# A hybrid gMLP and dilated-attention block on eight cores: reloading V in 5 transfers instead of 32 per head pair, with early weight loads gated by x and a reordered gating stage

## The chip, the cores and the metric

The kernel runs on all 8 cores of one Trainium2 chip. Each core does one of the 8 sequences of the batch with the same program; the cores exchange nothing. The metric is the device time of the slowest core in microseconds (us).

In these runs the program had a fast state and a slow one. In the slow state the cores of one die, or of both, showed a lower granted TensorE clock and the run took longer.

## The reference, cut to what matters

```python
# one block: x (8, 2048, 1024); 16 heads of 64; 8 gating groups of 128 channels; FF width 4096
h   = rms_norm(x, g1)
[u | v | q | k | v_attn | gate_a | gate_b] = h @ w_in
ya  = gelu(u) * (tril(W_s) @ layer_norm(v) + b_s)         # by chunks of 128 tokens
yb  = mixture of 3 dilated causal windows (128,1) (512,4) (2048,16) with ALiBi,
      weighted by their softmax denominators
m   = sigmoid(gate_a) * (ya @ w_a) + sigmoid(gate_b) * (yb @ w_b)
x1  = x + rms_norm(m @ w_o, g2);  out = x1 + rms_norm(relu(rms_norm(x1, g3) @ w1)**2 @ w2, g4)
```

(The activation and gate forms are abridged.) The three windows need V with the keys on the partitions in three different orders. The kernel projects V once per two head pairs, stores it in DRAM, and reads it back in two more orders: V0 for dilation 1, V1 for dilation 4. Dilation 16 uses the order in which it was projected.

## The kernel before

A helper records all operations; a scheduler orders them for each engine by priorities and by a cost given to each operation. That is why nearly all TensorE work has one line in the profile, and why new cost numbers move instructions.

The store of V and the reload for a head pair, 16 + 16 transfers of 48 KB:

```python
vscr_d = nc.dram_tensor("v_scr", [4, 128, 16, 384], BF16).ap()
...
P.dma("sp", lambda e, q=q: e.dma_start(out=vscr_d[pr][:, 4 * q:4 * q + 4, :], in_=stg[d][...]), ...)
...
def load_v(hp, prio):
    d, pr, hh = hp % 2, hp // 2, hp % 2
    src = vscr_d[pr]
    for a in range(4):
        s = src.rearrange("(n m) (c a) x -> a m c n x", n=4, a=4)[a]
        for c in range(4):       # V1: 16 transfers
            fns.append(... out=V1[d][32 * a:32 * a + 32, 4 * c:4 * c + 4, :], in_=s[:, c, :, 192 * hh:192 * hh + 192] ...)
    P.dma("sp", fns, 786e3, f"v1_{d}", rd, [V1[d].key()], prio=prio)
    s0 = src.rearrange("(b m) t x -> b t m x", m=8)
    for b in range(16):          # V0: 16 transfers
        fns.append(... out=V0[d][:, b, :], in_=s0[b][:, :, 192 * hh:192 * hh + 192] ...)
    P.dma("sp", fns, 786e3, f"v0_{d}", rd, [V0[d].key()], prio=prio)
```

The weights of the last MLP are turned into bf16 while attention runs: 24 transfers from DRAM to DRAM, 8 of w1 (2 MB in, 1 MB out) and 16 of w2 (half of that each). They are dealt evenly by number over the 32 slots of attention (8 head pairs times 4):

```python
for f in range(8):
    its.append(... P.dma("pool", ... dma_start(out=w1s_d[f], in_=w1_d[f]) ..., after=P.ops[-1]))
for f in range(16):
    its.append(... P.dma("pool", ... dma_start(out=w2s_d[f], in_=w2_d[f]) ..., after=P.ops[-1]))
...
for _ in range((nconv * (4 * hp + c + 1)) // 32 - (nconv - len(conv))):
    conv.pop(0)()
```

The softmax here doesn't subtract the row's maximum and nothing guards it: scores larger than these inputs give would overflow.

## Time and profile before

Before the change the median of three runs was 1358.19 us (1352.44 to 1365.54). The profiled run took 1348.16 us. It was one of the quicker ones. Its slowest core is core 5 with a span of 1346.6 us; the cores span 1323.8 to 1346.6 us.

| what (before, slowest core) | us |
|---|---|
| TensorE busy | 1191.2 of 1346.6 |
| TensorE waits for V from DRAM | 43.1 |
| start, until the QK projection of the last tiles begins (mean of cores) | 72.9 |
| one wait for the gating's reload | 15.9 |
| output projection stage (mean of cores) | 149.4 |

The page of the kernel before, first the TensorE line of the busy times (busy us, share, instructions; PEld is the weight load), then the chain of work that ended last, by engine:

```profile
PE 1191.2 (88%) x7560; PEld 601.9 (45%) x7560; DVE 563.9 (42%) x1007; ACT 483.9 (36%) x857; POOL 59.2 (4%) x122
PE 67%; DMA 13%; SPq 6%; DVE 5%; issue 5%; ACT 3%; DVEq 0%; ACTq 0%; POOL 0%; POOLq 0%
```

TensorE bounds the kernel, but a fifth of the chain is transfers and the queue that issues them (SPq). The waits of TensorE, kernel before (what it did next, what it waited for: total us, times, longest):

```profile
PE pst L195 <- DMA sb_V_0_50<-v_scr: 36.4, 3, 20.0
PE pst L199 <- DVE sb_xn_92 L486: 16.4, 4, 7.9
PE pst L195 <- DMA sb_gc<-gc_scr: 15.9, 1, 15.9
PE pst L195 <- DVE sb_xo_148 L926: 8.4, 2, 6.6
PE pst L195 <- DMA sb_V_1_51<-v_scr: 6.7, 1, 6.7
PE pst L195 <- DMA sb_w_6_144<-w_bf: 4.8, 1, 4.8
```

Two lines are waits for V (43.1 us). They ended at 122, 168, 228 (the one of 20.0 us) and 378 us. The issuing queue of the kernel before, from its timeline (start us, us from first to last issue, engine, line, operation, count). Line 577 is V1, line 583 is V0; the first two rows belong to head pair 0, the last two to head pair 2:

```profile
101.44 8.29 SPq L577 DMA_DIRECT2D sb_V_0_52<-v_scr  x16
109.78 10.43 SPq L583 DMA_DIRECT2D sb_V_0_50<-v_scr  x16
181.58 34.72 SPq L577 DMA_DIRECT2D sb_V_0_52<-v_scr  x16
216.35 9.91 SPq L583 DMA_DIRECT2D sb_V_0_50<-v_scr  x16
```

For head pair 0 the 32 issues take 19 us and V0 was usable at 122. For head pair 2 sixteen issues took 35 us: something else held the queue up. The reload also waits for the stores of V that it reads. The last of them before head pair 2 was issued at 154.6 us and landed only 26.8 us later (KB, us from issue to landing):

```profile
v_scr<-sb_stgV_49 SPq DMA_DIRECT2D x1, 384.0 KB, 26.8
```

### The profile page before, as it was taken

Reading aid. Unit: us, or ns where it says so; the run is one execution under the profiler, and the core shown is the slowest. Engines: PE = TensorE matmul, PEld = TensorE weight load, DVE = VectorE, ACT = ScalarE, POOL = GpSimd, SP = SyncE. Lnnn points to the kernel's source line nnn. Section 1 sums busy time; section 2 is a strip of 40 time slices with the busy share of each in tenths; the row PEclk is TensorE's granted clock in tenths of the full one; section 3 lists DMA queues with packets and bytes.
Section 4 is the critical chain, followed back from the end, with each engine's and each line's share of the span. In section 5 each row is a group of like instructions: output and inputs, shape, how many; then the busy total and the mean of one; then the engine's idle time right before and its main releaser. Section 6 shows DMA issues by size and latency. Waiting matters only on the chain.

```text
span 1346.6 us, 20587 instructions; the slowest of 8 cores (1323.8 to 1346.6 us)
## 1 busy us (share of the span) xinstructions
PE 1191.2 (88%) x7560; PEld 601.9 (45%) x7560; DVE 563.9 (42%) x1007; ACT 483.9 (36%) x857; POOL 59.2 (4%) x122
## 2 busy tenths in 40 slices
PE   2587794999967997799999996998999999999997
PEld 1264462666534433444444442443444444444443
DVE  3545662777745651643223235683122122212212
ACT  3524562666756523121222224574113213212311
POOL 0000000000000221000000011000000000000000
PEclk9798996999978999899999997998999999999999
DMA  9334986866774468221311129455010021011001
GB/s 226 108 88 86 120 137 117 165 138 125 141 147 72 102 169 168 64 64 32 63 32 32 32 78 349 167 182 193 32 64 32 0 79 47 1 63 63 1 32 63
DMA packets 67109, 130.44 MB, mean 97 GB/s; under 512 B 40641, under 2 KB 40769, under 8 KB 64450
## 3 DMA queue, kind: packets, MB, share of 16 engines
q0 software_dynamic: 9536, 54.53, 20.8%
q1 hardware_dynamic: 57474, 74.59, 18.9%
q8 instruction: 62, 1.02, 0.3%
q14 instruction: 37, 0.30, 0.1%
HBM read 139.58 MB, written 44.04 MB: 136 GB/s over the span
## 4 chain that ended last, share of the span: by engine, by line
PE 67%; DMA 13%; SPq 6%; DVE 5%; issue 5%; ACT 3%; DVEq 0%; ACTq 0%; POOL 0%; POOLq 0%
PE pst L195 66%; SPq L577 4%; DMA v_scr<-sb_stgV_49 3%; DMA gc_scr<-sb_gct_123 2%; SPq L583 2%; DMA gc_scr<-sb_gct_125 2%; DMA sb_xt_89<-x 2%; DMA sb_xo_148<-x 1%; DVE sb_ybT L705 1%; DMA sb_V_0_50<-v_scr 1%; PE pst L199 1%; DMA sb_gc<-gc_scr 1%; DMA x_scr<-sb_xo_148 1%; DMA v_scr<-sb_stgV_48 1%; DMA sb_w_6_144<-w_bf 1%
## 5 line engine op out<-in xcount | busy, mean ns | idle before, releaser
L195 PE MATMUL pst<-sb_w_146,sb_hid 128*128 128x512 bf16 x1024 | 221.7, 379 | 2.7 <-issue 1.4
L195 PEld LDWEIGHTS pst<-sb_w_146,sb_hid 128*128 128x128 bf16 x1024 | 100.0, 98 | 124.0 <-issue 3.7
L968 ACT ACTIVATE sb_hid<-pst 128x512 bf16<-128x512 f32 x128 | 76.4, 597 | 136.5 <-PE pst L195 135.9
L969 DVE TENSOR_TENSOR sb_hid<-sb_hid 128x512 bf16<-128x512 bf16 x128 | 54.2, 424 | 144.8 <-ACT sb_hid L968 142.1
L982 ACT ACTIVATE sb_junk_162<-pst 128x512 bf16<-128x512 f32 x32 | 19.1, 597 | 197.6 <-PE pst L195 197.6
L629 ACT ACTIVATE sb_Et_82<-pst 128x1024 bf16<-128x1024 f32 (+1 forms) x54 | 52.0, 962 | 65.7 <-PE pst L195 59.0
L195 PE MATMUL pst<-sb_hT,sb_wqk_62 128*128 128x512 bf16 x256 | 67.0, 412 | 4.9 <-ACT sb_hT L496 2.7
L195 PE MATMUL pst<-sb_wout,sb_merged 128*128 128x512 bf16 x256 | 60.4, 391 | 8.4 <-DVE sb_xo_148 L926 8.4
L629 ACT ACTIVATE sb_Et_84<-pst 128x1024 bf16<-128x1024 f32 (+1 forms) x53 | 51.2, 965 | 39.4 <-PE pst L195 33.6
L195 PE MATMUL pst<-sb_wva,sb_hT 128*128 128x512 bf16 x256 | 59.8, 393 | 5.5 <-ACT sb_gv_121 L782 4.7
L195 PE MATMUL pst<-sb_hT,sb_wqk_63 128*128 128x512 bf16 x256 | 62.9, 391 | 0.4 <-DVE sb_stgV_49 L561 0.2
L629 ACT ACTIVATE sb_Et_83<-pst 128x1024 bf16<-128x1024 f32 (+1 forms) x53 | 51.8, 977 | 24.9 <-PE pst L195 18.9
L195 PE MATMUL pst<-sb_hT,sb_wg_129 128*128 128x512 bf16 x256 | 57.9, 379 | 0.0
L195 PE MATMUL pst<-sb_hT,sb_wg_130 128*128 128x512 bf16 x256 | 57.9, 379 | 0.0
L195 PEld LDWEIGHTS pst<-sb_wout,sb_merged 128*128 128x128 bf16 x256 | 25.1, 100 | 39.9 <-issue 13.9
L195 PEld LDWEIGHTS pst<-sb_wva,sb_hT 128*128 128x128 bf16 x256 | 25.3, 101 | 38.1 <-issue 11.7
L195 PEld LDWEIGHTS pst<-sb_hT,sb_wqk_62 128*128 128x128 bf16 x256 | 24.6, 104 | 38.9 <-issue 18.8
L826 ACT ACTIVATE sb_yaT<-pst 128x512 bf16<-128x512 f32 x32 | 18.9, 599 | 56.6 <-PE pst L195 56.6
L195 PEld LDWEIGHTS pst<-sb_hT,sb_wg_130 128*128 128x128 bf16 x256 | 25.0, 98 | 30.2
L195 PEld LDWEIGHTS pst<-sb_hT,sb_wg_129 128*128 128x128 bf16 x256 | 25.0, 98 | 30.0
L195 PEld LDWEIGHTS pst<-sb_hT,sb_wqk_63 128*128 128x128 bf16 x256 | 23.6, 100 | 29.9 <-issue 7.1
L878 ACT ACTIVATE sb_sg_0_134<-pst,sb_small 128x512 f32<-128x512 f32 x16 | 11.0, 687 | 71.9 <-PE pst L195 71.9
(389 smaller groups left out, 1910.4 us busy)
## 6 DMA issues: line engine op xcount, KB each, us to landing
w_bf<-w POOLq DMA_DIRECT2D x8, 1024.0 KB, 17.7
w_bf<-w POOLq DMA_DIRECT2D x16, 512.0 KB, 9.0
sb_w_146<-w_bf POOLq DMA_DIRECT2D x16, 512.0 KB, 21.3
sb_xo_148<-x SPq DMA_DIRECT2D x8, 512.0 KB, 4.7
sb_gc<-gc_scr SPq DMA_DIRECT2D x16, 256.0 KB
sb_xo_149<-x SPq DMA_DIRECT2D x8, 512.0 KB, 4.8
sb_wg_129<-w_g POOLq DMA_DIRECT2D x4, 1024.0 KB, 8.5
sb_wg_130<-w_g POOLq DMA_DIRECT2D x4, 1024.0 KB, 8.2
```

The source lines that it names most:

```text
L195: e.matmul(out, lhsT=l, rhs=r, start=st, stop=sp, skip_group_check=True))
L199: fns = [lambda e, a=a, b=b: e.transpose(out=a, in_=b, identity=ident) for a, b in outs_ins]
L577: fns.append(lambda e, a=a, c=c, s=s: e.dma_start(out=V1[d][32 * a:32 * a + 32, 4 * c:4 * c + 4, :], in_=s[:, c, :, 192 * hh:192 * hh + 192]))
L583: fns.append(lambda e, b=b: e.dma_start(out=V0[d][:, b, :], in_=s0[b][:, :, 192 * hh:192 * hh + 192]))
L629: P.act(lambda e: e.activation(out=et[:, :, 0:W], in_=psall[:, sb:sb + 2, 0:W], func=AF.Exp, scale=0.125), 2 * W, [], [et.key()], [sb, sb ...
L705: P.dve(lambda e, hh=hh, lo=lo: e.tensor_tensor(out=ybT[lo:lo + 64, hp, 512 * c:512 * c + 512], in0=psr(bks[hh], lo, lo + 64), in1=lr[lo:l ...
L826: P.act(lambda e, bk=bk, g=g, w=w: e.activation(out=yaT[:, g, 512 * w:512 * w + 512], in_=ps(bk), func=AF.Gelu_apprx_tanh), 512, [], [yaT. ...
L878: P.act(lambda e, j=j, cb=cb, po=po, s_=s_: e.activation(out=s_[j][:], in_=ps(po + j), func=AF.Tanh, scale=0.5, bias=small[:, bg_c + 8 * j ...
L968: P.act(lambda e, fb=fb, bk=bk: e.activation(out=hid[:, fb, :], in_=ps(bk), func=AF.Relu), 512, [], [hid.key(fb)], [bk])
L969: P.dve(lambda e, fb=fb: e.tensor_tensor(out=hid[:, fb, :], in0=hid[:, fb, :], in1=hid[:, fb, :], op=ALU.mult), 512, [hid.key(fb)], [hid.k ...
L982: P.act(lambda e, hf=hf, bb=bb, s_=s_: e.activation(out=junk4[:, 0:512], in_=ps(bb[hf]), func=AF.Square, accum_out=s_[:, 8 + hf:9 + hf]), ...
```

## The change

It has four parts. The intent of each:

1. **V.** The scratch layout in DRAM changes so that V0 is read in 4 transfers and V1 in 1. The key orders inside a block change with it (`kk0`, `k1`), so the reordering copies of K and the bias tables do too; the copies into KT1 (K in the order for dilation 4) move from VectorE to ScalarE. V0 is loaded first.
2. **Start.** Eight x buffers instead of five; two of the early weight loads and the first bias table wait for x tiles; all copies of the transposed x (hT) go to VectorE.
3. **Output projection.** Each w2 load waits for a tile of the output projection; w1 slice 6 gets a place that frees earlier.
4. **Order.** New cost numbers; conversions and bias loads tied to a slot's last product (`anchor`); the first gating products one group later; the reload of V gets another priority.

The diff, cut to its core:

```diff
-            cost += max(n / 2400.0 + 0.0025, 0.1 if slow else 0.03)
+            cost += max(n / 2400.0 + 0.0025, 0.055) * (0.55 if slow else 1.0)
   ... (other cost numbers of ScalarE, VectorE and the queues likewise)
-    vscr_d = nc.dram_tensor("v_scr", [4, 128, 16, 384], BF16).ap()
+    vscr_d = nc.dram_tensor("v_scr", [4, 4, 128, 4, 384], BF16).ap()
   ...
+    NX, NXN = 8, 4            # x and normalised-x buffers, were 5 and 3
   ...
-    load_wv(0, -1970.0)
-    load_wqk(1, -1900.0)
+    load_wv(0, -1970.0, gate[5])
+    load_wqk(1, -1900.0, gate[13])
   ...
-            its.append(lambda f=f: P.dma("pool", ... w1s_d[f] ..., after=P.ops[-1]))
+            its.append(lambda f=f: P.dma("pool", ... w1s_d[f] ..., after=anchor[0]))
   ...
-                    P.dve(lambda e, o1=o1, s=s: e.tensor_copy(out=o1, in_=s.rearrange("p (a n m) -> p a n m", a=4, n=4)), ...
+                    P.act(lambda e, o1=o1, s=s: e.activation(out=o1, in_=s, func=AF.Copy), 512, [kk],
+                          [KT1[d].key((512 * w, 512 * w + 512))])
   ...
-        (load_v: 16 + 16 transfers, shown above)
+        src = vscr_d[pr].rearrange("c m a x -> (c m a) x")[:, 192 * hh:192 * hh + 192]
+        s0 = src.rearrange("(c b q) x -> c q b x", c=4, q=32)
+        P.dma("sp", [lambda e, c=c: e.dma_start(out=V0[d][32 * c:32 * c + 32, :, :], in_=s0[c]) for c in range(4)], 786e3, f"v0_{d}", rd,
+              [V0[d].key()], prio=prio)
+        P.dma("sp", lambda e: e.dma_start(out=V1[d][:], in_=src.rearrange("(b p) x -> p b x", p=128)), 786e3, f"v1_{d}", rd, [V1[d].key()],
+              prio=prio + 1)
   ...
-            P.prio = U0 + 10 * g + 5 + n4
+            P.prio = U0 + 10 * g + (5 if g else 21) + n4
   ...
-    W1OFF = [160, 168, 192, 144, 152, 128, 176, 184]
+    W1OFF = [160, 168, 192, 144, 152, 128, 136, 184]
   ...
-              [P.nkey(("w2s", q))], [w2.key((2 * q, 2 * q + 2))], prio=F0 + 20 + q)
+              [P.nkey(("w2s", q))], [w2.key((2 * q, 2 * q + 2))], prio=F0 + 20 + q, after=fgate[q])
```

More of the change, by code (lines that the diff above doesn't have):

```diff
@@ L200, in tr, with act @@
         return self._add("pe", fns, 0.06 * len(fns), reads, [self.bank(b) for b in banks], prio, lat=0.17, name=name)
-    def act(self, fn, n, reads, writes, banks=(), prio=None, name=""):
-        return self._add("act", [fn], 0.2 + n / 1200.0, reads, list(writes) + [self.bank(b) for b in banks], prio, lat=0.04, name=name)
+    def act(self, fn, n, reads, writes, banks=(), prio=None, name="", acc=False):
+        return self._add("act", [fn], (0.4 if acc else 0.11) + n / 1200.0, reads, list(writes) + [self.bank(b) for b in banks], prio, lat=0.04, name=name)
     def dve(self, fn, n, reads, writes, banks=(), prio=None, name="", rate=1):
-        return self._add("dve", [fn], 0.065 + n / (960.0 * rate), reads, list(writes) + [self.bank(b) for b in banks], prio,
+        return self._add("dve", [fn], 0.09 + n / (960.0 * rate), reads, list(writes) + [self.bank(b) for b in banks], prio,
                          lat=0.04, name=name)
@@ L214, in dma @@
             fns = [fns]
-        cost = (0.06 if q != "pool" else 1.0) * len(fns)
+        cost = (0.45 if q != "pool" else 0.7) * len(fns)
         o = self._add(q, list(fns), cost, reads, writes, prio, nb=nbytes, chan=chan, lat=2.0, name=name)
@@ L433, in build_nc @@
     Lr = [buf(f"Lr{i}", (199 + 2 * i) * K, [512], F32) for i in range(2)]
-    xt = [buf(f"xt{i}", (165 + 4 * i) * K, [1024], F32) for i in range(5)]
-    xn = [buf(f"xn{i}", (185 + 2 * i) * K, [1024]) for i in range(3)]
-    junk = buf("junk", 193 * K, [1024])
-    gbc = buf("gbc", 199 * K, [1024], F32)
-    grow = buf("grow", 195 * K, [1024], F32)
-    ones1 = buf("ones1", 203 * K, [128], F32)
+    NX, NXN = 8, 4
+    xt = [buf(f"xt{i}", (165 + 4 * i) * K, [1024], F32) for i in range(NX)]
+    xn = [buf(f"xn{i}", (88 + 2 * i) * K, [1024]) for i in range(NXN)]
+    junk = buf("junk", 96 * K, [1024])
+    gbc = buf("gbc", 98 * K, [1024], F32)
+    grow = buf("grow", 102 * K, [1024], F32)
+    ones1 = buf("ones1", 106 * K, [128], F32)
     hTw = [hT.key(None, (512 * w, 512 * w + 512)) for w in range(4)]
@@ L451, in build_nc @@
     P.dve(lambda e: e.memset(ones1[0:1, :], 1.0), 64, [], [ones1.key()])
+    P.act(lambda e: e.activation(out=stat[:, 63:64], in_=stat[:, 62:63], func=AF.Exp), 1, [stat.key((62, 63))], [stat.key((63, 64))], prio=-3000)
     P.dma("sp", lambda e: e.dma_start(out=grow[0:1, :], in_=gains_d[0:1, :]), 4e3, "c2", [], [grow.key()], prio=-2001)
@@ L456, in build_nc, with load_wqk, load_eb, load_wv @@
               [gbc.key((512 * hf, 512 * hf + 512))], [6 + hf])
-    def load_wqk(hp, prio):
+    def load_wqk(hp, prio, after=None):
         d = hp % 2
         P.dma("pool", lambda e: e.dma_start(out=wqk[d][:].rearrange("p k c -> p (k c)"), in_=wqk_d[hp]), 1e6, f"wqk{d}", [],
-              [wqk[d].key()], prio=prio)
-    def load_eb(hp, prio):
+              [wqk[d].key()], prio=prio, after=after)
+    def load_eb(hp, prio, after=None):
         d = hp % 2
         P.dma("sp", lambda e: e.dma_start(out=EB[d][:].rearrange("p a c -> p (a c)"), in_=eb_d[hp]), 0.33e6, f"eb{d}", [], [EB[d].key()],
-              prio=prio)
-    def load_wv(pr, prio):
+              prio=prio, after=after)
+    def load_wv(pr, prio, after=None):
         d = pr % 2
         P.dma("pool", lambda e: e.dma_start(out=wvb[d][:].rearrange("p k c -> p (k c)"), in_=wv_d[pr]), 1e6, f"wvb{d}", [],
-              [wvb[d].key()], prio=prio)
+              [wvb[d].key()], prio=prio, after=after)
     XORD = list(range(16))
+    gate = {}
     for n, i in enumerate(XORD):
-        b = n % 5
+        b = n % NX
         pr = -2000.0 + 10 * n
-        kx, kn = xt[b].key(), xn[n % 3].key()
+        kx, kn = xt[b].key(), xn[n % NXN].key()
         ks, kr = stat.key((i, i + 1)), stat.key((16 + i, 17 + i))
         P.dma("sp", lambda e, b=b, i=i: e.dma_start(out=xt[b][:], in_=toks(x_d, i)), 512e3, f"x{b}", [], [kx], prio=pr)
-        P.act(lambda e, b=b, i=i: e.activation(out=junk[:], in_=xt[b][:], func=AF.Square, accum_out=stat[:, i:i + 1]), 1024,
-              [kx], [junk.key(), ks], prio=pr)
+        sq = P.act(lambda e, b=b, i=i: e.activation(out=junk[:], in_=xt[b][:], func=AF.Square, accum_out=stat[:, i:i + 1]), 1024,
+              [kx], [junk.key(), ks], prio=pr, acc=True)
+        gate[n] = sq
         P.act(lambda e, i=i: e.activation(out=stat[:, 16 + i:17 + i], in_=stat[:, i:i + 1], func=AF.Ln, scale=1.0 / DM, bias=EPS), 1,
@@ L485, in build_nc @@
               [kr], [kr], prio=pr)
-        P.dve(lambda e, b=b, n=n, i=i: e.scalar_tensor_tensor(out=xn[n % 3][:], in0=xt[b][:], scalar=stat[:, 16 + i:17 + i], in1=gbc[:],
+        P.dve(lambda e, b=b, n=n, i=i: e.scalar_tensor_tensor(out=xn[n % NXN][:], in0=xt[b][:], scalar=stat[:, 16 + i:17 + i], in1=gbc[:],
                                                               op0=ALU.mult, op1=ALU.mult), 1024, [kx, kr, gbc.key()], [kn], prio=pr)
@@ L489, in build_nc @@
         pbf = ps(bk).bitcast(BF16)
-        P.tr([(pbf[:, 128 * kc:128 * kc + 128], xn[n % 3][:, 128 * kc:128 * kc + 128]) for kc in range(8)], ident[:],
+        P.tr([(pbf[:, 128 * kc:128 * kc + 128], xn[n % NXN][:, 128 * kc:128 * kc + 128]) for kc in range(8)], ident[:],
              [kn, kid], [bk], prio=pr)
-        if n % 2 == 0:
-            P.dve(lambda e, i=i, pbf=pbf: e.tensor_copy(out=hT[:, :, 128 * i:128 * i + 128], in_=pbf.rearrange("p (k t) -> p k t", k=8)), 1024,
-                  [], [hTt[i]], [bk], prio=pr)
-        else:
-            P.act(lambda e, i=i, pbf=pbf: e.activation(out=hT[:, :, 128 * i:128 * i + 128], in_=pbf.rearrange("p (k t) -> p k t", k=8),
-                                                       func=AF.Copy), 1024, [], [hTt[i]], [bk], prio=pr)
+        P.dve(lambda e, i=i, pbf=pbf: e.tensor_copy(out=hT[:, :, 128 * i:128 * i + 128], in_=pbf.rearrange("p (k t) -> p k t", k=8)), 1024,
+              [], [hTt[i]], [bk], prio=pr, rate=2)
     load_wqk(0, -1985.0)
-    load_wv(0, -1970.0)
-    load_wqk(1, -1900.0)
+    load_wv(0, -1970.0, gate[5])
+    load_wqk(1, -1900.0, gate[13])
     for i in range(2):
@@ L507, in conv_items @@
         for f in range(8):
-            its.append(lambda f=f: P.dma("pool", lambda e: e.dma_start(out=w1s_d[f], in_=w1_d[f]), 3e6, f"cv{f % 2}", [], [P.nkey(("w1s", f))], after=P.ops[-1]))
+            its.append(lambda f=f: P.dma("pool", lambda e: e.dma_start(out=w1s_d[f], in_=w1_d[f]), 3e6, f"cv{f % 2}", [], [P.nkey(("w1s", f))], after=anchor[0]))
         for f in range(16):
-            its.append(lambda f=f: P.dma("pool", lambda e: e.dma_start(out=w2s_d[f], in_=w2_d[f]), 1.5e6, f"cv{f % 2}", [], [P.nkey(("w2s", f))], after=P.ops[-1]))
+            its.append(lambda f=f: P.dma("pool", lambda e: e.dma_start(out=w2s_d[f], in_=w2_d[f]), 1.5e6, f"cv{f % 2}", [], [P.nkey(("w2s", f))], after=anchor[0]))
         return its
@@ L539, in proj_qk @@
                 if dst is KT:
-                    s = KT[d][:, 512 * w:512 * w + 512]
-                    o0 = KT0[d][:].rearrange("p (b t m) -> p t b m", b=16, t=16)[:, 4 * w:4 * w + 4]
-                    o1 = KT1[d][:, 512 * w:512 * w + 512].rearrange("p (n a m) -> p a n m", n=4, a=4)
-                    P.dve(lambda e, o0=o0, s=s: e.tensor_copy(out=o0, in_=s.rearrange("p (a b m) -> p a b m", a=4, b=16)), 512, [kk],
-                          [k0key(d, w)], rate=2)
-                    P.dve(lambda e, o1=o1, s=s: e.tensor_copy(out=o1, in_=s.rearrange("p (a n m) -> p a n m", a=4, n=4)), 512, [kk],
-                          [KT1[d].key((512 * w, 512 * w + 512))], rate=2)
+                    s = KT[d][:, 512 * w:512 * w + 512].rearrange("p (a m) -> p a m", a=4)
+                    o0 = KT0[d][:].rearrange("p (b t m a) -> p t a b m", b=16, t=4, a=4)[:, w]
+                    o1 = KT1[d][:, 512 * w:512 * w + 512].rearrange("p (m a) -> p a m", a=4)
+                    P.dve(lambda e, o0=o0, s=s: e.tensor_copy(out=o0, in_=s.rearrange("p a (b m) -> p a b m", b=16)), 512, [kk], [k0key(d, w)])
+                    P.act(lambda e, o1=o1, s=s: e.activation(out=o1, in_=s, func=AF.Copy), 512, [kk],
+                          [KT1[d].key((512 * w, 512 * w + 512))])
     def proj_v(pr, rng, pos):
@@ L564, in proj_v @@
                 q = i2 // 2
-                P.dma("sp", lambda e, q=q: e.dma_start(out=vscr_d[pr][:, 4 * q:4 * q + 4, :],
+                P.dma("sp", lambda e, q=q: e.dma_start(out=vscr_d[pr, q],
                                                        in_=stg[d][:, 4 * q:4 * q + 4, :, :].rearrange("p t h c -> p t (h c)")),
@@ L570, in load_v @@
         d, pr, hh = hp % 2, hp // 2, hp % 2
-        src = vscr_d[pr]
+        src = vscr_d[pr].rearrange("c m a x -> (c m a) x")[:, 192 * hh:192 * hh + 192]
         rd = [P.nkey(("vscr", pr, q)) for q in range(4)]
-        fns = []
-        for a in range(4):
-            s = src.rearrange("(n m) (c a) x -> a m c n x", n=4, a=4)[a]
-            for c in range(4):
-                fns.append(lambda e, a=a, c=c, s=s: e.dma_start(out=V1[d][32 * a:32 * a + 32, 4 * c:4 * c + 4, :],
-                                                               in_=s[:, c, :, 192 * hh:192 * hh + 192]))
-        P.dma("sp", fns, 786e3, f"v1_{d}", rd, [V1[d].key()], prio=prio)
-        fns = []
-        s0 = src.rearrange("(b m) t x -> b t m x", m=8)
-        for b in range(16):
-            fns.append(lambda e, b=b: e.dma_start(out=V0[d][:, b, :], in_=s0[b][:, :, 192 * hh:192 * hh + 192]))
-        P.dma("sp", fns, 786e3, f"v0_{d}", rd, [V0[d].key()], prio=prio)
+        s0 = src.rearrange("(c b q) x -> c q b x", c=4, q=32)
[3 more added lines that the diff above has]
+              prio=prio + 1)
+    anchor = [None]
     sctr, p0ctr, p12ctr, ectr, lctr = [0], [0], [0], [0], [0]
@@ L616, in s_job @@
                     n0, nn = 128 * n, 128
-                mms.append((psall[:, sb + hh, n0:n0 + nn], kk, qq, n == 0, n == len(blocks) - 1, nn, False))
+                mms.append((psall[:, sb + hh, n0:n0 + nn], kk, qq, n == 0, n == len(blocks) - 1, nn, True))
         W = n0 + nn
@@ L693, in pv_class @@
                             p2t[:, hh, 128 * a:128 * a + 128], False, a == 3, 128, False))
-        P.pe(mms, [stg[sd].key((4 * c, 4 * c + 4)), p2t.key()], bks, name="pv2")
+        anchor[0] = P.pe(mms, [stg[sd].key((4 * c, 4 * c + 4)), p2t.key()], bks, name="pv2")
         P.prio = prio - 20
@@ L713, in build_nc @@
     load_v(0, -1500.0)
-    load_eb(0, -1600.0)
+    load_eb(0, -1600.0, gate[9])
     for hp in range(NHP):
@@ L717, in build_nc @@
         if hp < NHP - 1:
-            load_eb(hp + 1, b0 + 50)
+            load_eb(hp + 1, b0 + 50, anchor[0])
             if hp < NHP - 2:
@@ L732, in build_nc @@
                 proj_qk(hp + 1, lambda i, n, b0=b0: b0 + 12 * i)
-                load_v(hp + 1, b0 + 60)
+                load_v(hp + 1, b0 + (15 if hp % 2 == 0 else 40))
             for _ in range((nconv * (4 * hp + c + 1)) // 32 - (nconv - len(conv))):
@@ L903, in build_nc @@
     h2T = merged
+    fgate = {}
     for i in range(16):
@@ L913, in build_nc @@
                   for kc in range(8)], km + [wout.key()], [bb[hf]], name="oproj")
+            fgate[i] = P.ops[-1]
             P.act(lambda e, hf=hf, bb=bb, s_=s_: e.activation(out=junk3[:, 0:512], in_=ps(bb[hf]), func=AF.Square,
-                                                              accum_out=s_[:, hf:hf + 1]), 512, [], [junk3.key(), s_.key((hf, hf + 1))], [bb[hf]])
+                                                              accum_out=s_[:, hf:hf + 1]), 512, [], [junk3.key(), s_.key((hf, hf + 1))], [bb[hf]], acc=True)
         P.dve(lambda e, s_=s_: e.tensor_tensor(out=s_[:, 2:3], in0=s_[:, 0:1], in1=s_[:, 1:2], op=ALU.add), 1, [s_.key((0, 2))],
@@ L930, in build_nc @@
         P.act(lambda e, x_=x_, s_=s_, n_=n_: e.activation(out=n_[:], in_=x_[:], func=AF.Square, accum_out=s_[:, 5:6]), 1024, [kx],
-              [n_.key(), s_.key((5, 6))])
+              [n_.key(), s_.key((5, 6))], acc=True)
         P.act(lambda e, s_=s_: e.activation(out=s_[:, 6:7], in_=s_[:, 5:6], func=AF.Ln, scale=1.0 / DM, bias=EPS), 1, [s_.key((5, 6))],
@@ L952, in build_nc @@
         P.dma("pool", lambda e, q=q: e.dma_start(out=w2[:, 2 * q:2 * q + 2, :].rearrange("p f c -> p (f c)"), in_=w2s_d[q]), 0.5e6, f"w2_{q}",
-              [P.nkey(("w2s", q))], [w2.key((2 * q, 2 * q + 2))], prio=F0 + 20 + q)
+              [P.nkey(("w2s", q))], [w2.key((2 * q, 2 * q + 2))], prio=F0 + 20 + q, after=fgate[q])
     gfin = buf("gfin", 200 * K, [1024], F32)
-    xi = [buf(f"xi{i}", (136 + 4 * i) * K, [1024], F32) for i in range(2)]
+    xi = [buf(f"xi{i}", (176 + 4 * i) * K, [1024], F32) for i in range(2)]
     junk4 = buf("junk4", 204 * K, [512])
@@ L983, in build_nc @@
                                                                   accum_out=s_[:, 8 + hf:9 + hf]), 512, [], [junk4.key(), s_.key((8 + hf, 9 + hf))],
-                      [bb[hf]])
+                      [bb[hf]], acc=True)
             P.dve(lambda e, s_=s_: e.tensor_tensor(out=s_[:, 10:11], in0=s_[:, 8:9], in1=s_[:, 9:10], op=ALU.add), 1, [s_.key((8, 10))],
@@ L1022, in _consts @@
     q0 = (16 * m16 + (t // 4) + 4 * (t % 4)).reshape(-1)
-    a, m32 = np.meshgrid(np.arange(4), np.arange(32), indexing="ij")
-    k1 = (4 * m32 + a).reshape(-1)
+    c_, m8_, a_ = np.meshgrid(np.arange(4), np.arange(8), np.arange(4), indexing="ij")
+    kk0 = (16 * m8_ + c_ + 4 * a_).reshape(-1)
+    k1 = np.arange(128)
     a, m64 = np.meshgrid(np.arange(4), np.arange(64), indexing="ij")
@@ L1031, in _consts @@
         o = 0
-        for dil, kk, qq in ((1.0, k0, q0), (4.0, k1, q1), (16.0, k2, q2)):
+        for dil, kk, qq in ((1.0, kk0, q0), (4.0, k1, q1), (16.0, k2, q2)):
             delta = (qq[None, :] - kk[:, None]).astype(np.float64)
```

## The prediction

> **What bounds the kernel now.** The page of the slowest core shows a span of 1346.6 us with TensorE busy 1191.2 us (88%); the chain of waits is 67% TensorE, 13% DMA, 6% the SP queue. From 566 to 807 and 952 to 1340 us TensorE is nearly always busy. The change can only win its idle time (155 us) and the half-clock time after that (mean clock 0.951). TensorE's timeline puts the idle time in five places:
> 1. Start, 0 to 74 us: TensorE mostly waits for normalised x tiles. The x tiles share the DMA with four weight loads; the first three are usable at 13.9, 18.9 and 23.7 us.
> 2. Waits for reloaded V: 9.2 us at 122, 6.7 at 168, 20.0 at 228, 7.3 at 378: 43 us.
> 3. The gating reload, 15.9 us at 547.
> 4. The output projection, 807 to 850: some 16 us, the chain running through an x1 store (8.7 us) and an x reload (9.1 us) while w2 loads.
> 5. w1 slice 6, 4.8 us at 933.
>
> **What the change does.**
> - V: 32 issues of 48 KB per head pair become 5. The SP timeline shows 8.3 + 10.4 us to issue the first 32 (0.52 to 0.65 us each). Packets stay 384 B, 4096 per head pair; at their measured 30 ns on 16 engines that is about 8 us (estimate). V0, now first, should land 6 to 10 us after its first issue, not 20.5. That removes the waits at 122, 168 and 378: 23 us, and about 8 us of half clock.
> - The 20 us wait is different. At 190 to 215 us the SP queue moved almost nothing, because three weight conversions with 32 KB packets (about 4.4 us each) held the engines. [...] 28 packets of 384 B in 195 to 200 us. The conversions stay, and come sooner as TensorE stalls less. I count on half: 11 us.
> - Start: two of four early weight loads wait for x tiles; x gets 8 buffers. Then x comes at about 1.7 us a tile (128 packets of 210 ns, 16 engines), and VectorE bounds: 1.28 + 0.69 us a tile with all hT copies there, plus about 0.5 for casts. All hT near 56 to 62 us instead of 74: 14 us.
> - KT1 copies move to ScalarE [...] ; both engines have slack. Cost: 0.
> - Gating: in the built order the first gating products follow 4 u groups, before 4.25. The wait is for gc's stores and reloads, which are untouched. Gain 0.
> - Output projection: w2 loads paced by it: 6 us. w1 slice 6 moves to the wout space, but slices 5 and 6 both wait for the last projection, some 6 us before use: 2 us.
>
> **Sum.** 14 + 31 + 11 + 8 = 64 us: **1294 us**, 8 in 10 between 1268 and 1322. Chances: faster 0.94, same 0.05, slower 0.01.
>
> **Signs.** Right: V waits in the waits view under 12 us in total, the last left about head pair 2; first V-projection matmul near 60 us; TensorE still waiting 12 to 18 us for gc; w1 slice 5 or 6 waiting under 4 us.
>
> **What would make it wrong.** Descriptors, not issues, limiting V; conversions starving V store and loads more, as they come closer together; VectorE stalling the start; the gating wait really shrinking.

No term of the sum is cut: it came to 14 + 31 + 11 + 8 = 64 us, so 1294, with a cost of 0 for the copies and a gain of 0 for the gating. That 0 for the copies, and the half of the 20 us wait, are estimates.

What the rest stands on, in the trace of before: the granted clock was 0.50 after the waits for V, from 122.0 to 127.9, 168.0 to 172.3 and 378.0 to 383.9 us, and half of these 16.1 us comes to the "8 us of half clock"; it was 0.50 also from 228.0 to 233.7. From 190 to 215 us the packets of the conversions' queue took 98.4% of the time of the 16 engines and those of V's queue 3.1%. And the "about 0.5 for casts" is what eight casts of 0.69 us and eight copies of 0.29 us in the start come to on each of 16 tiles.

## More of the kernel before

The busy times by stretch, for head pairs 2 and 3 before (window; its length; busy us and instructions of PE, PEld, DVE, ACT, POOL; granted clock of TensorE; share of the 16 DMA engines; GB/s):

```profile
166.00:220.00 54.00, 38.73 (x416) 24.29 (x416) 28.17 (x53) 25.45 (x32) 2.04 (x4) 0.88 0.85 135
220.00:258.00 38.00, 29.71 (x353) 20.45 (x354) 17.95 (x31) 19.67 (x26) 1.06 (x2) 0.82 0.68 139
```

The DMA engines are 85% and 68% busy here although they move only 135 to 139 GB/s (one slice of the same page, at 9 tenths busy, moves 349).

## The result and the profile after

The changed kernel took 1316.86 us (median of 4 runs, 1313.46 to 1318.86). The kernel before took 1359.55 us (median of 4) in the same rounds. The ratio is 0.9685, with a 95% interval of 0.9632 to 0.9739. Ratios here are the mean time of one kernel's fast runs over that of the other's of the same rounds, so they are not quite the ratios of the medians quoted.

The medians differ by 42.7 us, but the two profiled runs differ less, 1348.16 to 1318.77 us. The mean over the eight cores goes from 1334.7 to 1309.8 us, 24.9 us less. In five later sessions the fast runs of before had means over cores of 1335.7 to 1339.8 us; the four runs of after give 1308.3. So the body of the kernel gained some 27 to 31 us. The rest of the 42.7 is that the slowest core of before lay further above its mean (12 us in the profile, against 7 after) and that its timed runs of that session were on the long side (1359.3 us on average, against 1346 to 1354 in the later ones). Terms of the prediction are compared with the means of the cores in the two profiles, which leave less to the luck of one core.

The page of the kernel after, the same two lines as before:

```profile
PE 1189.8 (90%) x7560; PEld 601.4 (46%) x7560; DVE 571.7 (43%) x983; ACT 513.6 (39%) x882; POOL 59.4 (5%) x122
PE 75%; DMA 11%; ACT 4%; DVE 4%; issue 4%; SPq 1%; POOL 0%; DVEq 0%; ACTq 0%; POOLq 0%
```

TensorE's work is the same. The issuing queue has all but left the chain (6% to 1%). The waits of TensorE after:

```profile
PE pst L195 <- DMA sb_gc<-gc_scr: 16.8, 1, 16.8
PE pst L195 <- issue: 11.1, 5, 4.3
PE pst L195 <- DMA sb_V_0_52<-v_scr: 7.7, 1, 7.7
PE pst L195 <- DVE sb_xo_152 L921: 5.4, 2, 3.5
PE pst L195 <- DMA sb_w_5_147<-w_bf: 4.6, 1, 4.6
```

One wait for V is left, 7.7 us, ending at 199.6, in head pair 2. Over all eight cores the waits named for V fall from 36.6 us a core to 9.8. The issuing queue after, first two rows head pair 0, last two head pair 2 (line 573 is V0, line 575 V1):

```profile
96.14 1.92 SPq L573 DMA_DIRECT2D sb_V_0_50<-v_scr  x4
98.11 0.80 SPq L575 DMA_DIRECT2D sb_V_0_52<-v_scr  x1
159.78 10.79 SPq L573 DMA_DIRECT2D sb_V_0_50<-v_scr  x4
170.62 3.05 SPq L575 DMA_DIRECT2D sb_V_0_52<-v_scr  x1
```

Issuing fell from 19 us to 2.8. In head pair 2 four issues still stretched over 10.8 us, and V1, issued at 170.6, landed at 199.5. The stretches for head pairs 2 and 3 after, and what the transfers in 145 to 239 us took from issue to landing (KB each, median us):

```profile
145.00:193.00 48.00, 40.65 (x449) 25.80 (x445) 31.10 (x55) 32.47 (x40) 2.04 (x4) 0.93 1.02 147
193.00:239.00 46.00, 38.39 (x404) 23.93 (x404) 26.17 (x46) 27.98 (x34) 2.26 (x4) 0.89 0.89 146
w_bf<-w POOLq DMA_DIRECT2D x5, 1024.0 KB, 16.0
sb_V_0_50<-v_scr SPq DMA_DIRECT2D x4, 192.0 KB, 14.6
sb_V_0_52<-v_scr SPq DMA_DIRECT2D x1, 768.0 KB, 28.9
```

The DMA engines are now almost wholly busy (1.02 and 0.89) at 147 GB/s, with five weight conversions among their work. The store in front of the reload, issued at 133.9 us, is as late as before, so the reload of head pair 2 cannot start until 159.8:

```profile
v_scr<-sb_stgV_49 SPq DMA_DIRECT2D x1, 384.0 KB, 25.6
```

TensorE stood idle for 7.7 us in this wait for V, until 199.6. The granted clock is 0.50 around the end of that wait and 1.00 after it, as it is in 221 us of dense matmuls later on (552 to 773 us):

```profile
195.20:205.30 10.10, 5.68 (x33) 2.94 (x34) 0.69 (x1) 3.40 (x5) 0.00 (x0) 0.50 0.91 221
206.00:258.00 52.00, 46.88 (x535) 30.23 (x535) 37.34 (x65) 37.50 (x45) 3.81 (x7) 1.00 0.84 134
```

The KT1 copies, before on VectorE and after on ScalarE (busy us and mean ns of one after the bar, then the idle time before them):

```profile
L545 DVE COPY sb_KT_0_60<-sb_KT_56 128x512 bf16<-128x512 bf16 x16 | 4.6, 285 | 0.0
L544 ACT ACTIVATE sb_KT_0_60<-sb_KT_56 128x512 bf16<-128x512 bf16 x16 | 21.7, 1359 | 35.3 <-DVE sb_KT_56 L538 35.2
```

Time by stage, worked out from the trace's weight loads, mean of the eight cores of the profiled run. A head pair's row ends at its first product with V, so it holds the wait for that V. "to gating" runs from the last product of attention to the first gating product, "to gates" on to the first gate matmul, "oproj" from the output projection's first matmul to the MLP's second half. e1 to e12 are the experiments that follow, named by number.

```
             before  after    e1    e2    e3    e4    e5    e6    e7    e8    e9   e10   e11   e12
start          72.9   67.2  65.6  72.0  66.6  75.2  66.1  65.5  66.3  65.4  67.0  75.8  66.7  65.6
head pair 0    47.3   39.6  51.2  39.5  39.6  39.0  39.6  39.4  39.4  39.4  39.8  38.9  41.3  39.3
head pair 2    53.4   48.5  56.2  50.8  49.0  45.7  49.0  50.8  52.3  45.7  37.9  45.3  39.3  39.0
head pair 3    39.1   45.2  43.0  41.8  43.5  40.5  43.6  41.5  40.4  47.4  37.9  40.5  37.9  37.9
head pair 5    37.2   37.9  40.3  37.9  37.9  37.5  37.9  37.9  37.9  37.9  53.2  37.5  37.9  37.9
to gating      95.1   99.2  96.4 100.1  99.7  95.7 100.1  98.4  85.1  84.0 123.6  95.8  96.4  88.8
to gates       35.8   37.0  35.3  36.7  36.6  36.2  36.9  36.9  47.9  48.0  21.2  35.9  34.9  40.2
oproj         149.4  143.0 143.0 143.6 156.0 150.6 143.5 143.3 144.1 143.4 143.8 141.9 142.0 143.9
whole        1334.7 1309.8  1340  1313  1320  1312  1306  1305  1303  1302  1318  1302  1296  1290
```

From before to after, the start gives 5.7 us, head pair 0 gives 7.7, head pair 1 (not in the table: 44.7 to 37.5) 7.2, head pair 6 (36.9 to 35.5) 1.4, head pair 7 (41.0 to 36.2) 4.8 and the output projection 6.4. Head pairs 2 and 3 together go from 92.5 to 93.7 us, and the two gating rows lose 5.3. More matmuls fall into the stretch of head pairs 2 and 3 now (853 against 769 in the windows shown), so it does somewhat more work, but a later experiment does 828 of them in 76 us. A head pair that does not wait for V takes a little longer than before (head pair 5: 37.2 to 37.9).

### The profile page after: what moved, and what is told of

Its sections match the earlier page's. It is cut to its first block, busy times and chain, and to the rows that moved or that the text cites. A ratio compares the mean times of both kernels' runs of the same rounds, so it can differ in the third digit from the quotient of the medians.

```text
span 1317.2 us, 20425 instructions; the slowest of 8 cores (1300.5 to 1317.2 us)
## 1 busy us (share of the span) xinstructions
PE 1189.8 (90%) x7560; PEld 601.4 (46%) x7560; DVE 571.7 (43%) x983; ACT 513.6 (39%) x882; POOL 59.4 (5%) x122
## 3 DMA queue, kind: packets, MB, share of 16 engines
q8 instruction: 62, 1.02, 0.3%
## 4 chain that ended last, share of the span: by engine, by line
PE 75%; DMA 11%; ACT 4%; DVE 4%; issue 4%; SPq 1%; POOL 0%; DVEq 0%; ACTq 0%; POOLq 0%
PE pst L195 74%; DMA gc_scr<-sb_gct_127 4%; DMA sb_V_0_52<-v_scr 2%; DMA v_scr<-sb_stgV_49 2%; DMA sb_xt_87<-x 1%; PE pst L199 1%; SPq L573 1%; DVE sb_ybT L698 1%; DMA sb_w_5_147<-w_bf 1%; DMA sb_gc<-gc_scr 1%; ACT sb_Et_84 L622 1%; ACT sb_Lr_86 L693 1%; DMA sb_w_7_149<-w_bf 1%; ACT sb_Et_82 L622 1%; ACT sb_Et_83 L622 0%
## 5 line engine op out<-in xcount | busy, mean ns | idle before, releaser
L195 PEld LDWEIGHTS pst<-sb_hT,sb_wqk_62 128*128 128x128 bf16 x256 | 24.8, 105 | 40.2 <-issue 21.4
L871 ACT ACTIVATE sb_sg_0_138<-pst,sb_small 128x512 f32<-128x512 f32 x16 | 11.0, 688 | 71.9 <-PE pst L195 71.9
L195 PEld LDWEIGHTS pst<-sb_hT,sb_wg_134 128*128 128x128 bf16 x256 | 25.0, 98 | 30.3
L195 PEld LDWEIGHTS pst<-sb_hT,sb_wg_133 128*128 128x128 bf16 x256 | 25.0, 98 | 29.9
L871 ACT ACTIVATE sb_sg_0_136<-pst,sb_small 128x512 f32<-128x512 f32 x16 | 11.0, 688 | 69.8 <-PE pst L195 69.8
```

What stands on the lines that cost most here:

```text
L195: e.matmul(out, lhsT=l, rhs=r, start=st, stop=sp, skip_group_check=True))
L871: P.act(lambda e, j=j, cb=cb, po=po, s_=s_: e.activation(out=s_[j][:], in_=ps(po + j), func=AF.Tanh, scale=0.5, bias=small[:, bg_c + 8 * j ...
```

## The experiments

Twelve kernels were run in five sessions, all correct. e1 to e4 take the change apart. e5 to e8 test reasons for what was missing. e9 to e12 look into the largest one. The first four shared the runs of before with each other, as did the next four; each session ran on another chip. Spans of the same kernel differ by some us between runs, so differences of whole times under about 4 us are not read. Times are medians of fast runs.

### e1: the change without the V part

```diff
-"v_scr", [4, 4, 128, 4, 384]        +"v_scr", [4, 128, 16, 384]
-load_v: 4 + 1 transfers, kk0, k1    +load_v: 16 + 16 transfers, old K copies, k0, k1
```

> The kernel after, with V's reload alone undone: 32 issues per head pair, the old scratch layout and the old key orders (KT0 and KT1 copies on VectorE). Theory V (the five transfers carry most of the gain): 15 to 25 us slower than after (1332 to 1342 us), and waits for V of 7 to 20 us back at head pairs 0, 1 and 2. Rival S (the new cost numbers of the scheduler, that is the new order of instructions, carry the gain): within 6 us of after.

Measured: fast runs 1347.35, 1366.5 and 1351.91 us, ratio to before 1.0009 (0.9843 to 1.0175). Without the V part no gain shows, though the interval is wide. The start is still 7 us shorter than before, but head pair 0 grows to 51.2 and head pairs 2 and 3 to 99.2 us. The expected waits named for V did not come back in full: they are 4.2 us on the slowest core. The longest wait of TensorE there, 25.8 us in head pair 2, is put down to VectorE; the chain leads from it to a bias table, issued at 199.5 us behind 32 V issues that began at 160.6. So the 32 issues cost time also by what stands behind them in the queue.

### e2: the change without the start part

```diff
-NX, NXN = 8, 4 ; gate[...] on weight loads ; all hT copies on VectorE
+5 and 3 buffers ; no gates ; odd hT copies on ScalarE
```

> The kernel after, with the start alone undone: 5 x buffers, 3 xn buffers, no gated weight loads, odd hT copies on ScalarE. Theory V: 5 to 7 us slower than after, all of it before the last Q and K projection of head pair 0 (67.5 us after, mean of the cores; 73 expected here). If the new start costs something later (DMA pushed back), less than that.

Measured: 1319.43 us, ratio 0.9744 (0.9577 to 0.9911). The start row is 72.0 instead of 67.2, so the part wins 4.8 us there. At the end the profiles differ by 3 us (1313 to 1310), which is under the 4 us that are read; how much of the 4.8 the end keeps is not shown. Head pairs 2 and 3 still take 92.6 us here, without the early start.

### e3: the change without the output-projection part

```diff
-prio=F0 + 20 + q, after=fgate[q])   +prio=F0 + 20 + q)
-W1OFF[6] = 136, xi at 176           +W1OFF[6] = 176, xi at 136
```

> The kernel after, with the gate on the w2 loads and the place of w1 slice 6 undone. Theory: 5 to 7 us slower than after, all of it between the first output projection and the first second-layer matmul (142.9 us after, 149.2 before, mean of the cores). Rival: the w1 slice 5 wait of 4.6 us goes away here and the whole is within 2 us of after.

Measured: 1326.5 us, ratio 0.9793 (0.9677 to 0.9909). The stage is 156.0 us instead of 143.0, and the waits that the part had taken away are back. The waits of TensorE in e3:

```profile
PE pst L195 <- DVE sb_xo L921: 10.9, 2, 9.1
PE pst L195 <- DMA sb_w<-w_bf: 9.3, 1, 9.3
```

This part works as meant. Within the change it is worth 13 us in its stage, more than the 5 to 7 expected; against the kernel before the stage gained 6.4.

### e4: the kernel before with the V part alone

```diff
-"v_scr", [4, 128, 16, 384]           +"v_scr", [4, 4, 128, 4, 384]
-load_v: 16 + 16, k0, k1, K on DVE    +load_v: 4 + 1, kk0, new k1, KT1 copy on ScalarE
```

> The kernel before, with V's five transfers, the new scratch layout and key orders alone. Theory V: 18 to 28 us faster than before (1331 to 1341 us). Rival S: less than 8 us faster, as the old order and the old cost numbers stay.

Measured: 1319.62 us (1319.38 to 1320.81), ratio 0.9748 (0.966 to 0.9835). One part of four carries nearly the whole gain, more than the 18 to 28 us expected of it. It keeps the old priority of the reload, so that did not bring it. The waits of TensorE for V fell here too:

```profile
PE pst L195 <- DMA sb_V<-v_scr: 9.2, 2, 8.5
```

Beside the changed kernel, e4 starts 8.0 us later and needs less time in head pairs 2 and 3 (86.2 against 93.7 us). The early start is not what costs these 7.5 us, since e2, without it, takes 92.6. What e2 and e3 (92.5) have, and e4 and e10 (85.8) do not, is the new order, so the order is the likely cause; no run has it alone. And e4 starts later than before (75.2 against 72.9): with the old start, the new K copies seem to cost some 2 us.

### e5: conversions in packets of 4 KB

The prediction counted 28 packets of V among those of the conversions in 5 us (195 to 200 us of before). The author's theory was that V's packets stood behind the long ones; no trace or run shows in what order an engine takes them. If the 32 KB packets of the conversions kept V's 384 B packets waiting, smaller ones should help.

```diff
-w1_bf [8, 128, 4096], w2_bf [16, 128, 2048]
+w1_bf [8, 128, 2, 2080], w2_bf [16, 128, 2080]     # rows padded, so no packet joins two rows; [..., 0:2048] used
```

> The kernel after, with the same weight conversions at the same places, but written to padded scratch rows, so that their DMA packets are 4 KB and not 32 KB; the bytes stay. Theory packet (the V store and reload starve [...]): head pairs 1 to 3 shrink, the time from the first product with V of head pair 1 to that of head pair 3 falls from 93.7 us (mean of the cores) to 76 to 83, the gating wait by some us, the whole 12 to 20 us faster than after. Rival bandwidth (the DMA engines or the memory have no time left, whatever the packet): those 93.7 us stay within 3, and the whole too.

Measured: 1313.4 us, ratio 0.9704 (0.967 to 0.9739). Head pairs 2 and 3 take 92.6 us instead of 93.7, and the reloads stay slow. Transfers of e5 in 143 to 236 us (KB each, median us from issue to landing), and in the last line V1 of head pair 2 alone:

```profile
w_bf<-w POOLq DMA_DIRECT2D x5, 1024.0 KB, 17.7
sb_V<-v_scr SPq DMA_DIRECT2D x8, 192.0 KB, 8.6
sb_V<-v_scr SPq DMA_DIRECT2D x2, 768.0 KB, 26.2
sb_V<-v_scr SPq DMA_DIRECT2D x1, 768.0 KB, 44.5
```

The theory in its form, that the 32 KB matter, falls: V1 of head pair 2 needed 44.5 us, not less than 28.9. The same bytes take about as much engine time: in these stretches a packet of 32 KB took 4.4 us on average, one of 4 KB 0.5 us (weight loads among them), and both are long beside V's 0.03 us. That leaves a rival open: V may still stand behind packets of 4 KB. e5 cannot tell that from engines that have no time left (their packets took 85.8% of the time of the 16 engines in 143 to 236 us), and no run made the packets equal.

### e6: the KT1 copies of head pair 0 back on VectorE

In the start after the change, ScalarE stands in front of each KT1 copy and waits for VectorE, with the squares of the next x tiles behind it. Waits of ScalarE, 14 to 68 us, kernel after:

```profile
ACT sb_KT_0_60 L544 <- DVE sb_KT_56 L538: 20.1, 3, 8.4
```

```diff
-P.act(activation(out=o1, in_=s, func=AF.Copy))
+P.dve(tensor_copy(out=o1, in_=s)) if hp == 0 else P.act(...)
```

> The kernel after, with the KT1 copies of head pair 0 alone back on VectorE. Theory queue (at the start ScalarE, in order, stands for 8.4, 6.0 and 5.7 us in front of such a copy, and the statistics of the next x tiles wait behind it): the last Q and K projection of head pair 0 starts 4 to 8 us sooner than in after (67.2 us). Rival VectorE (the start is bound by VectorE's own work): no sooner, or up to 2 us later. How much of it the end sees is open: the old start cost only 3 us of 4.8 there.

Measured: 1312.17 us, ratio 0.9703 (0.9672 to 0.9734). The 20 us of waiting are gone, but the start row only goes from 67.2 to 65.5 us. Nearly all of that idle time cost nothing. The likely reason is that VectorE and TensorE set the pace in turn (3.15 us a tile for the first four tiles), not ScalarE.

### e7: the first two gate-weight loads wait for the gating reload

```diff
-        P.dma("sp", ... gc reload)            +        glast = P.dma("sp", ... gc reload)
-              prio=G0 + 20 * cb - 30)         +              prio=G0 + 20 * cb - 30, after=glast if cb < 2 else None)
```

> The kernel after, with the first two gate weight loads (2 MB each) held back until the last reload of gc was issued and landed. Theory: these loads fall on gc's last stores (one store took 23 us), so the time from the end of attention to the first gating product falls from 99.2 to 86 to 93 us, 6 to 12 us faster in all. Rival: gc's chain is bound by itself (three buffers, reloads into eight partitions): within 3 us.

Measured: 1309.33 us, ratio 0.9669 (0.9626 to 0.9713). TensorE's wait for gc falls from 16.8 us to:

```profile
PE pst L195 <- DMA sb_gc<-gc_scr: 10.6, 1, 10.6
```

The row "to gating" shrinks from 99.2 to 85.1, but "to gates" grows from 37.0 to 47.9 us, because now the gate weights are late. Of 14 us, 11 come back as another wait. That fits two loads that compete for the same DMA time: moving one behind the other mostly moves the wait.

### e8: e5, e6 and e7 together

> The three of these at once. If the theories packet, queue and gc hold and do not overlap: 20 to 35 us faster than after, 1282 to 1297 us. If TensorE's other waits take over, less than the sum.

Measured: 1307.15 us (1306.61 to 1309.28), ratio 0.9669 (0.9649 to 0.969). The expected 20 to 35 us did not come: it is about 10 us faster than the changed kernel, and its ratio is that of e7 alone. Head pairs 2 and 3 still take 93.1 us. None of the three edits touched what held them.

### e9: no conversion in head pairs 0 to 2

```diff
-for _ in range((nconv * (4 * hp + c + 1)) // 32 - ...
+for _ in range((nconv * max(0, 4 * hp + c - 11)) // 20 - ...
```

> The changed kernel with one edit: no weight conversion (24 transfers to DRAM, float to half width) is started in head pairs 0 to 2; all 24 are spread over head pairs 3 to 7. In the changed kernel head pairs 2 and 3 together take 93.7 us (mean of the cores), against about 76 us for two later pairs, and TensorE waits there 7.7 us for one V buffer that needed 28.9 us from issue to landing. Theory A, the bytes of the conversions leave the DMA engines no time for the V stores and reloads of that stretch: head pairs 2 and 3 fall to 76 to 84 us, the reloads there land 6 to 12 us after issue, waits for V go under 4 us; later pairs may grow by 0 to 6 us, and the whole gains 5 to 12 us. Theory B, the late V comes from the order of the queue on the issuing engine (the store of the next pair's V, which waits for its projection, stands ahead of the reload): head pairs 2 and 3 stay within 3 us of 93.7, the wait for V within 2 us of 7.7, and the whole stays within 3 us of 1317.

Measured: 1324.93 us (1320.21 to 1326.21), ratio 0.98 (0.9741 to 0.9858). Head pairs 2 and 3 fall to 75.8 us, as theory A said, with no wait for V named on any of the eight cores. The same two stretches in e9 and the reloads issued in them (of head pairs 3 and 4, since that of head pair 2 now came earlier); then V1 of head pair 2 alone, issued at 142.3, and the store before it, issued at 133.4:

```profile
145.00:183.00 38.00, 36.16 (x415) 23.30 (x416) 28.43 (x50) 30.04 (x37) 0.53 (x1) 1.00 0.42 104
183.00:221.00 38.00, 36.12 (x413) 23.30 (x416) 28.50 (x50) 30.03 (x37) 1.29 (x2) 1.00 0.36 80
sb_V<-v_scr SPq DMA_DIRECT2D x8, 192.0 KB, 3.8
sb_V<-v_scr SPq DMA_DIRECT2D x2, 768.0 KB, 7.6
sb_V<-v_scr SPq DMA_DIRECT2D x1, 768.0 KB, 6.2
v_scr<-sb_stgV SPq DMA_DIRECT2D x1, 384.0 KB, 6.5
```

The DMA engines drop from 1.02 and 0.89 to 0.42 and 0.36, the clock is full (1.00), and V1 of head pair 2 lands in 6.2 us instead of 28.9. A good part of the delay was the store: it lands in 6.5 us instead of 25.6, and the reload is issued at 140.1 instead of 159.8. The order of the issuing queue is not the cause: the store of the next V still stands in the same place in it. The whole kernel, however, loses: the conversions now come at a higher rate later and hit head pair 5 (53.2 us instead of 37.9) and the gating (144.8 us for both rows instead of 136.2). The wait of VectorE in head pair 5 of e9, and the issue it waited for:

```profile
DVE sb_PT L634 <- DMA sb_EB<-eb: 14.7, 1, 14.7
269.84 17.33 SPq L467 DMA_DIRECT2D sb_EB<-eb  x1
```

There it is the bias table that comes late, behind V on the same queue. So theory A was right about the stretch and wrong about the sum: the expected gain of 5 to 12 us in the whole did not come; the median is 8 us longer.

### e10: the kernel before with the V part and the output-projection part

```diff
 e4, and:
-prio=F0 + 20 + q)                   +prio=F0 + 20 + q, after=fgate[q])
-W1OFF[6] = 176, xi at 136           +W1OFF[6] = 136, xi at 176
```

> The kernel before with two parts of the change alone: V in 5 transfers with its key orders, and the w2 loads behind the output projection's tiles with w1 slice 6 moved out of the way. Start, gates, cost numbers and order are those of before. Theory A, the parts add: the V part alone had a mean over cores of 1312.3 us in its profile and 1319.6 timed, the w2 part is worth 6 to 13 us at the output projection (150.6 to about 143 us for that stage): mean 1300 to 1306, timed 1307 to 1314, so a little faster than the changed kernel (1309.8 and 1316.9), because the rest of the change (start, new cost numbers, gating order) gives back in head pairs 2 to 4 and in the gating what it wins in the start. Theory B, the rest of the change is worth its 8 us in the start here too: timed 1320 or more.

Measured: 1311.64 us (1308.19 to 1317.09), ratio 0.972 (0.9642 to 0.9797). The mean over cores of its profile is 1301.5 us, against 1309.8 for the whole change. The parts add as theory A said. The start and the new order, which are all that the whole change has beyond this, show no gain at the end; in the profiles the kernel without them is 8 us ahead. Since the two were not run in the same rounds, the size of this lead is not settled.

### e11: conversions of equal size, at an even rate

e9 says that the conversions matter at the time of a reload. In the kernel, 24 conversions are dealt evenly by number, but the first eight carry twice the bytes. Cutting those in two makes 32 equal ones, one for each slot.

```diff
-its.append(... dma_start(out=w1s_d[f], in_=w1_d[f]) ...)
+for h in range(2):
+    its.append(... dma_start(out=w1s_d[f][:, 2048 * h:2048 * h + 2048], in_=w1_d[f][:, 2048 * h:2048 * h + 2048]) ...)
```

> The changed kernel with the eight w1 conversions (each twice the size of a w2 conversion) cut in halves, so that the 32 attention slots each start one conversion of the same size; the same bytes move, at an even rate over all eight head pairs instead of 1.6 times faster in the first three. The run with no conversion in head pairs 0 to 2 took 75.8 us for head pairs 2 and 3 instead of 93.7, but lost 15 us in head pair 5 and 8 us in the gating. Theory A, what counts is the conversion rate at the time of a V reload: head pairs 2 and 3 take 77 to 85 us, hp 4 to 7 grow by at most 4 us, the gating by at most 4 us, the mean over cores is 1295 to 1303 and the timed median 1301 to 1311. Theory B, one conversion in flight is enough to hold a reload up, whatever its size: head pairs 2 and 3 stay at 89 us or more and the timed median within 4 us of 1317.

(The "1.6 times" comes out as 1.4: 8.5 of 16 MB in three of eight head pairs.)

Measured: fast runs 1296.45 to 1314.71 us, median 1301.46, ratio 0.9661 (0.9613 to 0.9709). The mean over cores of the fast runs is 1293.4 us, against 1308.3 for the changed kernel. Head pairs 2 and 3 take 77.2 us, as theory A expected, and nothing is lost in head pair 5 or the gating; head pair 7 grows by 5 us (36.2 to 41.3; at most 4 were expected). In the profiled run, core 5, the slowest, had a granted clock of 0.81 from 108 to 187 us, and cores 4 and 5 had means of 0.953 and 0.947 over the whole run against 0.965 to 0.972 on the others, which lengthens head pairs 0 to 2 in the table; on cores 0 to 3 head pairs 2 and 3 take 75.9 us, as in e9. Transfers of e11 in 148 to 225 us:

```profile
w_bf<-w POOLq DMA_DIRECT2D x8, 512.0 KB, 7.7
sb_V<-v_scr SPq DMA_DIRECT2D x8, 192.0 KB, 4.9
sb_V<-v_scr SPq DMA_DIRECT2D x2, 768.0 KB, 11.1
```

No wait of TensorE for V is left on any core. Halving the columns also made the packets 4 KB; since e5 had those and did not gain there, the dealing is what helped. Two things changed in it, the smaller size of one conversion and the even spacing, and no run separates them. The mean share of the DMA engines does not explain it: on the slowest core of e11 it is 0.82 and 0.73 over the 77 us of these stretches (148 to 225), and on that of before it is 0.85 and 0.68 over 92 us (166 to 258). The two kernels were run in different sessions, between which the kernel before differed by up to 4 us in the mean over cores, so of the 15 us at least some 11 are the edit's. The ratios to before do not settle it: 0.9661 and 0.9685, with intervals that overlap.

### e12: e11 with two small edits

The KT1 copies of e6, and only the second of the gate-weight loads held back (`after=glast if cb == 1 else None`).

> The even conversions together with two small edits: head pair 0's KT1 copies on VectorE (alone: 1.7 us earlier last QK projection of the start) and only the second of the first two gate-weight loads held until the last key block of gc has been reloaded (both held: the wait for gc fell by 6 us, but the next stage grew by 11). If the edits add, the mean over cores of the fast runs goes from 1293.4 us to 1287 to 1291 and the timed median from about 1302 to 1295 to 1300; the stage before the gating products falls from 96.4 to 87 to 92 us and the next one stays within 4 us of 34.9. If the gate weights are needed as early as gc is, the two stages together stay within 2 us of 131.3 and the whole stays within 3 us of 1302.

Measured: 1299.56 us (1296.79 to 1303.54), ratio 0.9645 (0.9573 to 0.9717), mean over cores of the fast runs 1290.6 us. "To gating" falls from 96.4 to 88.8 and "to gates" grows from 34.9 to 40.2 (expected: at most 38.9), 129.0 us for both instead of 131.3. The mean is at the upper edge of what was expected, the two stages together only just outside "within 2 us". It has the lowest median and ratio. That it beats e11 is not shown: the intervals of the ratios overlap widely.

## Why the prediction was right or wrong, point by point

The prediction said 1294 us, with 1268 to 1322 for 8 times in 10, and 0.94 for faster by over 2%. The result, 1316.86 us, is inside the range and near its upper end. It is faster by over 2%. The sum of 64 us was too large; the medians gained 42.7, the means of the profiled cores 24.9.

- **V waits at 122, 168 and 378: 31 us.** The mechanism was right (e4: the V part alone gives 1319.62 us; e1: no gain without it). The waits are gone. The four pieces of V0 of head pair 0, first issued at 96.1, landed 4.6 us after issue in the median, and TensorE used them at 107.3; before, V0 was usable 20.5 us after the first issue. The three waits end in head pairs 0, 1 and 6, whose rows gave 7.7 + 7.2 + 1.4 = 16.3 us on the mean of the cores; head pair 7, right after, gave another 4.8. So the size was too large. The 31 had been read from the slowest core, whose waits for V were 43.1 us where the mean core's were 36.6.
- **The 20 us wait, counted half: 11 us.** This is the step that failed. "The conversions stay, and come sooner as TensorE stalls less. I count on half: 11 us." The named waits did fall, but the stage did not: head pairs 2 and 3 took 93.7 us instead of 92.5. In e4 the V part did win 6.3 us there, so the rest of the change, most likely its new order, took that back. The cause was in the prediction's own list of what might go wrong, and e9 and e11 show it: with the conversions gone from there, or dealt evenly, the same stage takes 75.8 and 77.2 us. A good part of the delay is not in the sum at all: the last store of V before head pair 2 took 25.6 us to land (26.8 before, 6.5 in e9). The prediction named the 32 KB packets; e5 shows that their size is not decisive. Whether it is the engine time of the conversions or something else about their packets stays open.
- **Start: 14 us.** Also mis-sized: 5.7 us on the mean (e2: 4.8); how much of it the end kept is not shown. All hT were expected "near 56 to 62 us"; the last QK projection began at 67.2 on the mean. The sum of VectorE's durations was right (1.28 + 0.69 us a tile), but TensorE and VectorE wait for each other in turn (3.15 us a tile for the first four), and each set of QK projections blocks that chain for 5.2 to 6.2 us.
- **KT1 to ScalarE: cost 0.** Small, but not 0. A KT1 copy took 1.36 us on ScalarE, where before it took 0.29 on VectorE, and a KT0 copy, still on VectorE, 0.74 us instead of 0.29. ScalarE waited 20.1 us in front of them in the start, but taking that away gave only 1.7 us (e6); with the old start e4 and e10 begin 2 to 3 us later than before.
- **Gating: gain 0.** It lost 5.3 us instead. The wait for gc stayed, 15.9 before and 16.8 after, as foreseen. e7 shows that holding the gate weights back for gc mostly trades one wait for the other.
- **Output projection: 8 us.** 6.4 us against before; e3 shows 13 within the changed kernel. The x reload has left the chain, as said. The sign "w1 slice 5 or 6 waiting under 4 us" was missed slightly: slice 5 waits 4.6.

Signs: waits for V of 7.7 us on the slowest core (said: under 12), the last in head pair 2 (said: about there), gc still 16.8 (said: 12 to 18). The first V projection began at 73.3 us on the slowest core, not near 60.

Open: TensorE stopped in the middle of groups of matmuls for up to 4.3 us in the changed kernel ("issue", 11.1 us in all). Transfers on the instruction queue, 16 KB each, fell within three of these stops or less than 1 us before them. The longest lies in head pair 2. That is a coincidence in time and was not tested. Why e10 and e2 lead or trail by a few us is not settled either. And head pair 7's 5 us in e11 were not looked into.

## What to carry to other kernels

When a transfer is late, look at what else the DMA engines carry in that stretch, and at the store that the transfer waits for, before counting on fewer issues: here fewer and larger transfers took head pairs 2 and 3 from 92.5 to some 86 us at best (e4, e10), and evenly dealt conversions to 77.2 (e11). Deal background transfers out by bytes, not by number; in e11 that won some 11 us or more in the mean over cores. And take a gain away from one stage only after checking who uses the same transfer time next; e7 and e9 each won 14 to 18 us in one stage and gave 11 or more back in another.
